# RWKV-7 mixer in a hybrid trunk: one 128x128 transpose for alpha and v, and two heads that alternate

## The chip, the cores and the metric

The kernel runs on one core of a Trainium2 chip. The metric is the device time of one execution in microseconds. Times are medians of several runs; the trace is of one profiled execution.

## The reference

One inference step of a trunk with two layers, for 1024 latent and 128 context tokens (1152 in all), model width 1024, float32. Each layer projects the normed input for four parallel groups of heads, joins their outputs in one projection, and ends with a squared-ReLU MLP. One of the groups is the RWKV-7 mixer, 4 heads of 64, run forward and backward over the tokens. Per token, with a state S (value x key) for each head, it is this scan:

```python
def step(S, inp):
    r_t, w_t, kk_t, a_t, kt_t, v_t = inp
    s_kk = jnp.einsum('bhvk,bhk->bhv', S, kk_t)
    S = (S * w_t[:, :, None, :] - s_kk[..., None] * (kk_t * a_t)[:, :, None, :]
         + v_t[..., None] * kt_t[:, :, None, :])
    return S, jnp.einsum('bhvk,bhk->bhv', S, r_t)
```

The other groups are a bidirectional SSD, neighbourhood attention and differential attention.

## The kernel before, in words

The mixer works in chunks of 64 tokens: 18 chunks, 16 latent and 2 context. Two heads share the 128 partitions (a head pair p, 64 channels each), so there are two pairs, two directions d and two layers: eight passes. `rwkv_first` builds for one pass the tiles A and B of 128 x 18 x 2 x 64 (of each chunk: in A alpha and the decayed r, in B beta and the decayed k) and the small triangular matrices Ti, which a solver on 72 partitions (lines 861 to 868, VectorE and GpSimd) inverts block by block and `rwkv_join` completes. `rwkv_second` is the pass itself. `prepare` takes a group of four chunks (the last group, of the context, has two), `scan` carries the state over them.

`prepare` runs, with PSUM tiles of one bank each from `ps3`: the transposes of v and of alpha into one bank (lines 930 and 931: v by a product with the identity into partitions 64 to 127, alpha by a transpose into partitions 0 to 63), emptied by ScalarE into R (lines 932, 933); for each head four products of B with A (line 938, the head's 64 partitions as contraction) into a bank of its own, masked by VectorE into E (line 939); the transposes of B (line 942); products of E with R (947), of R with Ti (952) and of E with R again (958), each emptied by ScalarE or VectorE. In float32 a product leaves two records, a transpose one.

`ps3` hands out tiles of a pool of two banks, and each third one from the pool `ps_e` of one bank, until that pool is given up after the first of a layer's four passes. `values` loads v of a head pair (128 x 1152) from scratch memory by SyncE's queue, once for both directions.

The program is written in an order, and a planner puts each engine's instructions in the order in which it expects them to be ready, earlier ones in the program first. So neighbourhood attention (`nat_core`, lines 1174 to 1257) and differential attention (`diff_core`, lines 1274 to 1380), which come later in the program, fill TensorE between the mixer's steps: their scores are lines 1231, 1232 and 1347, their transposes and value products lines 1129 and 1141. Each engine works through its own list in order.

Of the kernel before, what the change touches and what calls it, by code (L numbers as in the profile page):

```python
# [8 lines left out]
F32 = mybir.dt.float32  # L9
# [3 lines left out]
ALU = mybir.AluOpType  # L13
# [5 lines left out]
T = NS + NP_  # L19
# [11 lines left out]
def bcast_mid(ap, n):  # L31
    return ap.unsqueeze(1).to_broadcast([ap.shape[0], n, ap.shape[1]])
# [79 lines left out]
def ps2(env):  # L112
    return env.ps_d.tile([128, 512], F32, tag="d", name="psd")


def ps3(env):

    env.turnr += 1
    if env.ps_e is not None and env.turnr % 3 == 0:
        return env.ps_e.tile([128, 512], F32, tag="e", name="pse")  # L120
    return ps2(env)
# [567 lines left out]
def rwkv_core(env, u, a, b, st0, scr, yout, stout):  # L689

    nc, C = env.nc, env.const
    big = u.big2

    u.St = [[[[big.tile([128, 64], F32, name=f"st{q}{s}{h}{i}") for i in range(3)] for h in range(2)] for s in range(2)] for q in range(2)]
    for q in range(2):
        for s in range(2):
            for h in range(2):
                for i in range(3):
                    lo = 64 - 64 * h
                    nc.gpsimd.tensor_copy(u.St[q][s][h][i][lo:lo + 64, :], C.idst[lo:lo + 64, :])  # L700

    u.R = [big.tile([128, 4, 256], F32, name=f"R{i}") for i in range(2)]
    for r in u.R:
        nc.gpsimd.memset(r[64:128, :, 0:64], 0.0)
        nc.gpsimd.memset(r[64:128, :, 192:256], 0.0)
    u.turn = 0

    def values(p):
        u.vv = big.tile([128, T], F32, tag="vv", name="vv")
        nc.sync.dma_start(out=u.vv, in_=scr[7 + p])  # L710
        u.yf = big.tile([128, T], F32, tag="yf", name="yf", bufs=2)

    first = lambda p, d: rwkv_first(env, u, p, d, scr, ps3)
    join = lambda d, w: rwkv_join(env, u, d, w, ps3)
    second = lambda p, d, w, *between: rwkv_second(env, u, p, d, w, st0, stout, between)
    done = []
    step = lambda f: lambda: next(f)
    last = lambda f: lambda: done.append(next(f))
    values(0)
    f = first(1, 0)  # L720
    second(0, 0, a, (0, step(f)), (1, step(f)), (2, step(f)))
    join(1, b)
    next(f)
    env.ps_e = None
    g = first(1, 1)
    second(0, 1, b, (-1, last(f)), (0, step(g)), (1, step(g)), (2, step(g)))
    y0 = u.yf
    a = done.pop()
    join(0, a)
    next(g)  # L730
    b = next(g)
    values(1)
    second(1, 0, a)
    rwkv_out(env, u, 0, y0, u.pt, scr, yout)
    join(1, b)
    second(1, 1, b)
    env.wide = True
    rwkv_out(env, u, 1, u.yf, u.pt, scr, yout, psd)
# [137 lines left out]
def rwkv_join(env, u, d, work, ps):  # L876

    nc = env.nc
    Ti, dT, dTT = work[2], work[4], work[5]
    q = d * 32  # L880
    o = 32 - q
    TU = u.FT("TU", 1152)[0:64].rearrange("p (u x) -> p u x", x=32)
    nc.sync.dma_start(out=TU[q:q + 32], in_=dT[d * 36:d * 36 + 36].rearrange("u t j -> t u j"))
    for u0 in range(0, 36, 16):
        m = min(16, 36 - u0)
        um = lambda a, m=m: a.rearrange("p (u x) -> p u x", u=m)
        pp = ps(env)
        for i in range(m):
            nc.tensor.matmul(pp[o:o + 32, i * 32:i * 32 + 32], Ti[q:q + 32, u0 + i, o:o + 32], TU[q:q + 32, u0 + i], start=True, stop=True)
        nc.scalar.activation(out=TU[o:o + 32, u0:u0 + m], in_=um(pp[o:o + 32, :m * 32]), func=AF.Copy)  # L890
    for b in range(2):
        nc.sync.dma_start(out=Ti[b * 32:b * 32 + 32, :, b * 32:b * 32 + 32], in_=dTT[b * 36:b * 36 + 36].rearrange("u j t -> j u t"))
    for u0 in range(0, 36, 16):
        m = min(16, 36 - u0)
        um = lambda a, m=m: a.rearrange("p (u x) -> p u x", u=m)
        pp = ps(env)
        for i in range(m):
            nc.tensor.matmul(pp[q:q + 32, i * 32:i * 32 + 32], TU[o:o + 32, u0 + i], Ti[o:o + 32, u0 + i, o:o + 32], start=True, stop=True)
        nc.scalar.activation(out=Ti[q:q + 32, u0:u0 + m, o:o + 32], in_=um(pp[q:q + 32, :m * 32]), func=AF.Copy)


def rwkv_second(env, u, p, d, work, st0, stout, between=()):

    nc, C, big, yf = env.nc, env.const, u.big2, u.yf
    A, B, Ti, sc = work[:4]
    u.turn += 1
    St = u.St[u.turn % 2]
    for s in range(2):
# [14 lines left out]
    def prepare(gi):  # L923
        c0, m = groups[gi]
        R = u.R[gi % 2]
        E = big.tile([128, 2, 4, 192], F32, tag="E", name="E", bufs=2)
        cm = lambda a: a.rearrange("p (c x) -> p c x", c=m)
        pp = ps3(env)
        for i in range(m):
            nc.tensor.matmul(pp[64:128, i * 128:i * 128 + 128], u.vv[:, (c0 + i) * 64:(c0 + i) * 64 + 64], C.ident, start=True, stop=True)  # L930
            nc.tensor.transpose(pp[0:64, i * 128:i * 128 + 128], A[:, c0 + i, 0], C.ident)
        nc.scalar.activation(out=R[64:128, 0:m, 64:192], in_=cm(pp[64:128, :m * 128]), func=AF.Copy)
        nc.scalar.activation(out=R[0:64, 0:m].rearrange("p c (a x) -> p c a x", a=4)[:, :, 0:4:3], in_=pp[0:64, :m * 128].rearrange("p (c a x) -> p c a x", c=m, a=2), func=AF.Copy)
        for h in range(2):
            hs = slice(h * 64, h * 64 + 64)
            pp = ps3(env)
            for i in range(m):
                nc.tensor.matmul(pp[:, i * 128:i * 128 + 128], B[hs, c0 + i].rearrange("p a t -> p (a t)"), A[hs, c0 + i].rearrange("p a t -> p (a t)"), start=True, stop=True)  # L938
            nc.vector.tensor_tensor(out=E[:, h, 0:m, 0:128], in0=cm(pp[:, :m * 128]), in1=bcast_mid(C.mask[d], m), op=ALU.mult)
        pp = ps3(env)  # L940
        for i in range(m):
            nc.tensor.transpose(pp[:, i * 128:i * 128 + 128], B[:, c0 + i].rearrange("p a t -> p (a t)"), C.ident)
        nc.scalar.activation(out=E[:, :, 0:m, 128:192].rearrange("p h c x -> p c h x"), in_=pp[:, :m * 128].rearrange("p (c h x) -> p c h x", c=m, h=2), func=AF.Copy)
        pp = ps3(env)
        for i in range(m):
            for h in range(2):
                nc.tensor.matmul(pp[0:64, i * 128 + h * 64:i * 128 + h * 64 + 64], E[64:128, h, i, 0:64], R[64:128, i, 64 + h * 64:128 + h * 64], start=True, stop=True)
        nc.scalar.activation(out=R[0:64, 0:m, 64:192], in_=cm(pp[0:64, :m * 128]), func=AF.Copy)
        pp = ps3(env)
        for i in range(m):  # L950
            for h in range(2):
                nc.tensor.matmul(pp[h * 64:h * 64 + 64, i * 128:i * 128 + 128], Ti[:, h * 18 + c0 + i], R[:, i, h * 128:h * 128 + 128], start=True, stop=True)
        for h in range(2):
            nc.scalar.activation(out=R[0:64, 0:m, h * 128:h * 128 + 128], in_=cm(pp[h * 64:h * 64 + 64, :m * 128]), func=AF.Copy)
        for h in range(2):
            pp = ps3(env)
            for i in range(m):
                nc.tensor.matmul(pp[:, i * 128:i * 128 + 128], R[:, i, h * 128:h * 128 + 128], E[:, h, i, 64:192], start=True, stop=True)  # L958
            pv = cm(pp[:, :m * 128])
            z, w = slice(h * 64, h * 64 + 64), slice(64 - h * 64, 128 - h * 64)  # L960
            nc.vector.tensor_tensor(out=E[z, h, 0:m, 64:128], in0=pv[z, :, 0:64], in1=A[z, c0:c0 + m, 1], op=ALU.add)
            nc.vector.tensor_tensor(out=E[z, h, 0:m, 128:192], in0=pv[z, :, 64:128], in1=bcast_mid(C.idst[z], m), op=ALU.add)
            nc.scalar.activation(out=E[w, h, 0:m, 64:192], in_=pv[w], func=AF.Copy)
        return E
# [31 lines left out]
    def also(gi):  # L996
        for g, f in between:
            if g == gi:
                f()

    E = prepare(0)
    also(-1)
    for gi in range(5):
        nxt = prepare(gi + 1) if gi < 4 else None
        scan(gi, E)
        also(gi)
        E = nxt
# [725 lines left out]
```

## Time and profile before

| | |
|---|---|
| time, median of 3 runs | 4233.19 us (4231.91 to 4238.97) |
| time of the profiled execution | 4236.38 us |
| its span | 4234.6 us |
| TensorE busy | 4062.3 us, 96% of the span |
| VectorE busy | 2498.9 us, 59% |
| ScalarE busy | 1524.2 us, 36% |
| GpSimd busy | 1104.4 us, 26% |
| mean granted TensorE clock | 0.965 of 2.4 GHz |

A timeline row gives start, duration, engine, line, operation and tiles (written <- read) of one or several equal instructions in a row; in brackets stands the idle time of the engine before it and what ended it. PE is TensorE, DVE VectorE, ACT ScalarE, POOL GpSimd, SPq the queue of SyncE, which issues the DMAs. A product's duration includes its drain, so neighbours overlap; what it costs the engine's list is the distance from start to start.

### The profile page before, as it was taken

How to read it: one execution, taken by the hardware profiler on the slowest of the kernel's cores; microseconds unless marked ns; L12 is line 12 of the kernel's file. 1: busy time of each engine (PE TensorE's matmuls, PEld its weight loads, DVE VectorE, ACT ScalarE, POOL GpSimd, SP SyncE). 2: the span in 40 equal slices, each digit the busy share in tenths (PEclk: the TensorE clock that was granted, in tenths of full speed). 3: DMA queues.
4: the chain of work that ended last, by engine and by line, in shares of the span. 5: the costliest groups of instructions: out<-in, count | busy, mean ns of one | idle time of the engine just before them, and what ended most of it. 6: DMA issues, size and time to landing. Idle time of an engine off the chain costs nothing.

```text
span 4234.6 us, 69159 instructions
## 1 busy us (share of the span) xinstructions
PE 4062.3 (96%) x27394; PEld 3722.1 (88%) x27394; DVE 2498.9 (59%) x5734; ACT 1524.2 (36%) x2896; POOL 1104.4 (26%) x866
## 2 busy tenths in 40 slices
PE   8899889999989999999999999899999999999999
PEld 5889877777779999999998998778777999999999
DVE  4896747678675894333345756576877463333333
ACT  4333325556553212211243233355566241111111
POOL 2243340223133221111232433302322331211111
PEclk9999989989999999999999998999889999999999
DMA  6663343322221451111134333543221301111111
GB/s 196 199 199 112 121 133 76 84 64 68 54 96 54 145 169 60 40 46 40 41 110 147 119 127 95 143 97 83 41 60 46 135 26 40 43 42 40 45 41 70
DMA packets 222707, 375.74 MB, mean 89 GB/s; under 512 B 100960, under 2 KB 155760, under 8 KB 221360
## 3 DMA queue, kind: packets, MB, share of 16 engines
q1 hardware_dynamic: 222320, 371.31, 29.2%
q8 instruction: 216, 3.54, 0.4%
q14 instruction: 107, 0.88, 0.1%
q0 software_dynamic: 64, 0.02, 0.0%
HBM read 285.33 MB, written 86.42 MB: 88 GB/s over the span
## 4 chain that ended last, share of the span: by engine, by line
PE 77%; DVE 11%; DMA 5%; issue 2%; SPq 2%; ACT 2%; POOL 1%; DVEq 0%; ACTq 0%; POOLq 0%
PE psd L101 12%; PE psd L99 12%; PE psd L100 12%; PE tps L1141 5%; PE psx L101 5%; PE psx L99 5%; PE psx L100 5%; PE tps L1129 3%; PE S L1347 2%; DVE junk L162 2%; PE psd L938 1%; DVE tm L867 1%; PE psd L958 1%; PE psd L930 1%; DMA K<-scr 1%
## 5 line engine op out<-in xcount | busy, mean ns | idle before, releaser
L84 POOL TENSOR_TENSOR wl<-raw,wh 128x1024 fp32r<-128x1024 f32 (+3 forms) x200 | 474.2, 2372 | 1543.1 <-ACT wh L82 1520.5
L82 ACT ACTIVATE wh<-raw 128x1024 fp32r<-128x1024 f32 (+3 forms) x200 | 205.9, 1031 | 793.8 <-PE psd L101 672.7
L294 DVE SCALAR_TENSOR_TENSOR x<-psd,md,x 128x384 f32<-128x384 f32 (+2 forms) x442 | 212.5, 504 | 349.5 <-PE psd L101 346.0
L101 PE MATMUL psd<-fl,wh 128*128 128x384 f32 x992 | 335.2, 338 | 0.0
L99 PE MATMUL psd<-fh,wl 128*128 128x384 f32 x992 | 334.7, 337 | 0.0
L100 PE MATMUL psd<-fh,wh 128*128 128x384 f32 x992 | 334.6, 337 | 0.0
L99 PE MATMUL psd<-h2h,wl 128*128 128x384 f32 x816 | 283.5, 348 | 9.1 <-ACT st L262 6.2
L1141 PE MATMUL tps<-pT,V 128*64 128x128 f32 (+1 forms) x2144 | 287.8, 284 | 4.5 <-ACT pT L1136 3.7
L100 PE MATMUL psd<-h2h,wh 128*128 128x384 f32 x816 | 282.7, 347 | 0.0
L101 PE MATMUL psd<-h2l,wh 128*128 128x384 f32 x816 | 281.3, 346 | 0.0
L1141 PEld LDWEIGHTS tps<-pT,V 128*64 128x64 f32 (+1 forms) x2144 | 239.1, 141 | 36.2 <-issue 22.8
L379 DVE TENSOR_TENSOR fl<-s,fh 128x384 fp32r<-128x384 f32 x192 | 209.1, 1090 | 97.4 <-ACT fh L378 97.0
L1136 ACT ACTIVATE pT<-tps 128x512 f32<-128x512 f32 (+3 forms) x368 | 166.3, 475 | 173.6 <-PE tps L1129 160.6
L99 PE MATMUL psd<-h0h,wl 128*128 128x384 f32 x592 | 207.5, 350 | 0.8 <-ACT qx L1098 0.6
L377 DVE SCALAR_TENSOR_TENSOR s<-psd,r 128x384 f32<-128x384 f32 x128 | 71.2, 556 | 231.2 <-ACT r L376 230.8
L99 PE MATMUL psd<-h1h,wl 128*128 128x384 f32 x592 | 205.3, 347 | 2.4 <-ACT h1h L244 2.0
L100 PE MATMUL psd<-h0h,wh 128*128 128x384 f32 x592 | 204.9, 346 | 0.0
L100 PE MATMUL psd<-h1h,wh 128*128 128x384 f32 x592 | 204.3, 345 | 0.0
L101 PE MATMUL psd<-h0l,wh 128*128 128x384 f32 x592 | 203.8, 346 | 0.0
L101 PE MATMUL psd<-h1l,wh 128*128 128x384 f32 x592 | 202.2, 343 | 0.1
L294 DVE SCALAR_TENSOR_TENSOR x<-psx,md,x 128x384 f32<-128x384 f32 (+2 forms) x198 | 103.4, 538 | 160.6 <-PE psx L101 160.2
L1353 ACT ACTIVATE e<-e,st 128x1280 f32<-128x1280 f32 x144 | 180.5, 1253 | 47.4 <-DVE st L1352 40.6
(613 smaller groups left out, 11021.3 us busy)
## 6 DMA issues: line engine op xcount, KB each, us to landing
raw<-in_w_ff_dram SPq DMA_DIRECT2D x128, 512.0 KB
mod<-in_w_mod_dram SPq DMA_DIRECT2D x80, 512.0 KB
raw<-in_w_in_fm_dram SPq DMA_DIRECT2D x42, 512.0 KB
scr<-st SPq DMA_DIRECT2D x78, 192.0 KB
scr<-x SPq DMA_DIRECT2D x26, 576.0 KB
K<-scr SPq DMA_DIRECT2D x32, 352.0 KB
K<-scr SPq DMA_DIRECT2D x64, 176.0 KB
u<-scr SPq DMA_DIRECT2D x18, 576.0 KB
```

The lines of the kernel that those rows point to most:

```text
L82: nc.scalar.activation(out=h[:, :n], in_=raw, func=AF.Copy)
L84: nc.gpsimd.tensor_tensor(out=l[:, :n], in0=raw, in1=h[:, :n].bitcast(F32), op=ALU.subtract)
L99: nc.tensor.matmul(ps, al, bh, start=i == 0, stop=False)
L100: nc.tensor.matmul(ps, ah, bh, start=False, stop=False)
L101: nc.tensor.matmul(ps, ah, bl, start=False, stop=i == n - 1)
L162: nc.vector.scalar_tensor_tensor(out=junk, in0=w[:, i * 512:i * 512 + 512], scalar=0.5, in1=parts[c * 2 + i], op0=ALU.mult, op1=ALU.mult, ...
L294: env.nc.vector.scalar_tensor_tensor(out=x[:, kt, s0:s1], in0=ps[:, s0 - c0:s1 - c0], scalar=g[:, kt, cd:cd + 1], in1=x[:, kt, s0:s1], op0 ...
L379: nc.vector.tensor_tensor(out=fl[j][:, c0:c0 + n], in0=s, in1=fh[j][:, c0:c0 + n].bitcast(F32), op=ALU.subtract)
L1129: nc.tensor.transpose(pp[0:n, i * 128:i * 128 + 128], e[:, o:o + n], C.ident)
L1136: nc.scalar.activation(out=pT[0:g[i][1], i * 128:j * 128], in_=pp[0:g[i][1], i * 128:j * 128], func=AF.Copy)
L1141: nc.tensor.matmul(out, V[0:n, vb], parts[k // 4][0:n, k % 4 * 128:k % 4 * 128 + 128], start=k == 0, stop=k == len(kt) - 1)
L1353: nc.scalar.activation(out=e[:, :N], in_=e[:, :N], func=AF.Exp, scale=-1.0, bias=m, accum_out=st[:, 6:7] if c else s0)
```

## The change

Alpha and v of a chunk stand side by side in one tile `av` of 128 x 18 x 2 x 64. v is loaded straight into its half; alpha is copied into the other half by GpSimd at the start of each pass, from A, which keeps its own. One transpose of 128x128 a chunk takes the place of the product and the transpose. The products of the two heads are issued in turn, chunk by chunk, into two banks that are taken together, and the two masks follow.

```diff
     def values(p):
-        u.vv = big.tile([128, T], F32, tag="vv", name="vv")
-        nc.sync.dma_start(out=u.vv, in_=scr[7 + p])
+        u.av = big.tile([128, 18, 2, 64], F32, tag="av", name="av")
+        nc.sync.dma_start(out=u.av[:, :, 1], in_=scr[7 + p].rearrange("p (c t) -> p c t", t=64))
...
     A, B, Ti, sc = work[:4]
+    av = u.av
+    nc.gpsimd.tensor_copy(av[:, :, 0], A[:, :, 0])
...
         for i in range(m):
-            nc.tensor.matmul(pp[64:128, i * 128:i * 128 + 128], u.vv[:, (c0 + i) * 64:(c0 + i) * 64 + 64], C.ident, start=True, stop=True)
-            nc.tensor.transpose(pp[0:64, i * 128:i * 128 + 128], A[:, c0 + i, 0], C.ident)
+            nc.tensor.transpose(pp[:, i * 128:i * 128 + 128], av[:, c0 + i].rearrange("p a t -> p (a t)"), C.ident)
...
+        pair = [ps3(env), ps3(env)]
+        for i in range(m):
+            for h in range(2):
+                hs = slice(h * 64, h * 64 + 64)
+                nc.tensor.matmul(pair[h][:, i * 128:i * 128 + 128], B[hs, c0 + i].rearrange("p a t -> p (a t)"), A[hs, c0 + i].rearrange("p a t -> p (a t)"), start=True, stop=True)
         for h in range(2):
-            hs = slice(h * 64, h * 64 + 64)
-            pp = ps3(env)
-            for i in range(m):
-                nc.tensor.matmul(pp[:, i * 128:i * 128 + 128], B[hs, c0 + i].rearrange("p a t -> p (a t)"), A[hs, c0 + i].rearrange("p a t -> p (a t)"), start=True, stop=True)
-            nc.vector.tensor_tensor(out=E[:, h, 0:m, 0:128], in0=cm(pp[:, :m * 128]), in1=bcast_mid(C.mask[d], m), op=ALU.mult)
+            nc.vector.tensor_tensor(out=E[:, h, 0:m, 0:128], in0=cm(pair[h][:, :m * 128]), in1=bcast_mid(C.mask[d], m), op=ALU.mult)
```

## Rows read from the trace of the kernel before

**Rows 1.** Both stretches: length; PE, PEld, DVE, ACT, POOL busy; clock; DMA share, GB/s

```profile
628.00:1250.00 622.00, 580.49 (x5001) 463.61 (x4999) 449.21 (x1168) 353.43 (x698) 140.14 (x151) 0.94 0.29 72
2694.00:3310.00 616.00, 579.58 (x5008) 464.06 (x5007) 453.46 (x1165) 353.83 (x696) 150.95 (x164) 0.93 0.32 79
```

**Rows 2.** The chain that ended last, shares by line, 628 to 1250 us

```profile
by line: PE tps L1141 16.9%; PE tps L1129 7.8%; PE S L1347 5.3%; PE psd L938 5.0%; issue 4.0%; PE psd L958 3.9%; PE psd L930 3.1%; DMA K<-scr 3.0%; PE psd L947 2.5%; PE S L1231 2.3%; PE psx L979 2.3%; PE psd L931 2.0%; PE S L1232 1.8%; PE p
```

**Rows 3.** TensorE's timeline in a group of layer 1's last pass

```profile
3211.09 0.43 PE L930 MATMUL psd<-pack,vv 128*64 128x128 f32 x2
...
3211.68 0.43 PE L930 MATMUL psd<-pack,vv 128*64 128x128 f32 x2
...
3212.86 1.16 PE L938 MATMUL psd<-A,B 64*128 64x128 f32 x8
3213.95 0.66 PE L1129 MATMUL tps<-pack,e 128*128 128x128 f32 x4
...
3215.34 1.16 PE L938 MATMUL psd<-A,B 64*128 64x128 f32 x8
3216.42 0.66 PE L942 MATMUL psd<-pack,B 128*128 128x128 f32 x4
3216.84 0.48 PE L1347 MATMUL S<-K,Q 128*128 128x512 f32 x1
```

**Rows 4.** TensorE's timeline, a group of two chunks with both heads together

```profile
2811.87 0.37 PE L938 MATMUL psd<-A,B 64*128 64x128 f32 x1
2811.89 0.37 PE L938 MATMUL pse<-A,B 64*128 64x128 f32 x1
...
2812.53 0.39 PE L1231 MATMUL S<-K,Q 128*128 128x256 f32 x1
```

**Rows 5.** TensorE's timeline, a group whose heads stand one behind the other

```profile
688.40 0.82 PE L938 MATMUL pse<-A,B 64*128 64x128 f32 x5
...
690.04 0.33 PE L942 MATMUL psd<-pack,B 128*128 128x128 f32 x1
```

**Rows 6.** ScalarE's timeline, the second eviction of the transposes of rows 3

```profile
3213.57 0.59 ACT L933 ACTIVATE R<-psd 64x512 f32<-64x512 f32 x1
```

**Rows 7.** Timeline at the start of layer 1's stretch: GpSimd, and the first transposes

```profile
2697.14 2.41 POOL L852 TENSOR_TENSOR A<-r,W 128x1152 f32<-128x1152 f32 x1
...
2699.61 8.28 POOL L700 COPY st<-pack 64x64 f32<-64x64 f32 x24
...
2708.70 0.31 POOL L705 MEMSET R<- 64x256 f32 x1
...
2710.22 0.69 PE L930 MATMUL pse<-pack,vv 128*64 128x128 f32 x2
...
2714.85 0.66 POOL L1211 COPY BI<-BT 128x576 f32<-128x576 f32 x1 [5.85 <-DMA BT<-scr]
```

**Rows 8.** Line 930 alone between passes: length, PE busy (records), clock, DMA

```profile
739.00:762.00 23.00, 0.00 (x0) 0.93 0.77 197
...
869.00:904.00 35.00, 0.00 (x0) 0.76 0.50 138
```

**Rows 9.** SyncE's timeline: issues of v's load and of a load in 256-byte runs

```profile
2697.92 0.57 SPq L710 DMA_DIRECT2D vv<-scr  x1
...
2700.78 0.60 SPq L1202 DMA_DIRECT2D V<-scr  x1
```

**Rows 10.** Longest pieces of layer 1's chain: start, us, what

```profile
2697.92 5.99 DMA vv<-scr
2703.93 10.78 DMA BT<-scr
```

**Rows 11.** Stretches of 40 us, columns as in rows 1

```profile
880.00:920.00 40.00, 33.11 (x343) 26.46 (x339) 28.42 (x86) 16.31 (x29) 6.35 (x6) 0.71 0.36 83
...
3160.00:3200.00 40.00, 40.00 (x362) 32.76 (x361) 31.76 (x82) 26.89 (x47) 7.15 (x6) 1.00 0.05 11
3200.00:3240.00 40.00, 36.72 (x336) 30.83 (x334) 25.72 (x69) 26.11 (x52) 5.78 (x4) 1.00 0.39 96
```

## Prediction

> **What bounds the kernel now.** The change touches two stretches, one in each layer, in which the RWKV mixer runs beside neighbourhood and differential attention: from its first transposed chunk to the last value products, 628 to 1250 us and 2694 to 3310 us. I read the busy time of each engine there first [rows 1]: TensorE is busy for 580.49 of 622 us and 579.58 of 616 us, so it stands idle for 41.5 and 36.4 us, 78 of 1238 us (6%). VectorE follows with 449 and 453 us. The reader is to see that no other engine comes near TensorE. Second, the chain of work that ended last [rows 2]: in layer 0's stretch it runs over TensorE's lines, attention's L1141 and L1129 first, with L938 at 5.0%, L930 at 3.1% and L931 at 2.0%. So these products of the mixer are not hidden work: they stand in one queue with attention's products. Third, the order of TensorE's instructions in time, because busy time counts the drain of each product beside the start of the next: what one costs the queue is the distance from its start to the next start [rows 3].
>
> **Part one: one transpose for two.** Now each chunk takes a product of v with the identity (two records) and a transpose of alpha; they repeat every 0.59 us (3211.09 to 3211.68; three such periods and a little reach to 3212.86) [rows 3]. There are 18 chunks, 4 passes (two head pairs, two directions) and 2 layers: 144 chunks, 144 x 0.59 = 85 us. After it a chunk is one 128x128 transpose against the identity. The same form stands at L942: four take 0.42 us from the first start to the next line's start (3216.42 to 3216.84), 0.105 us each [rows 3]. A group pays something for changing from one kind of product to another; I take 0.14 us a chunk, 20 us. Saved: 65 us of TensorE's queue. At the lower clock both grow alike, so that is no smaller there. The eviction by ScalarE stays: two instructions with the same shapes.
>
> **Part two: the heads alternate.** One head's four products (K 64, so half of the array's rows; two records each) hold the queue for 1.09 us (3212.86 to 3213.95), and the other head's for 1.08 (3215.34 to 3216.42) [rows 3]. Where both heads' products were ready together, they ran side by side already: in one group of two chunks the records start in pairs, 2811.87 and 2811.89, and both heads are through by 2812.53, 0.66 us with the change of kind at either end [rows 4]. Where one head's block stands right before the other's, they overlap in part: sixteen records in 1.64 us, 688.40 to 690.04 [rows 5]. So if the alternation reaches the engine, a group of four saves about 1.09 us and one of two about 0.44: 32 x 1.09 + 8 x 0.44 = 38 us, less some 4 us that such groups have now, 34. If it doesn't, 0. What decides is the second PSUM bank: the pair now wants two at once, and for most of the stretch (after ps_e is given up) the pool has two, of which the transposes just before hold one until ScalarE has emptied it, to 3213.57 + 0.59 = 3214.16, while the first head started at 3212.86 [rows 3, 6]. An order made by readiness would then run head 0's four products first. I take half, 17 us, and keep 0 and 34 for the range. VectorE's two masks come after both heads instead of one after each; the first waits longer by one head's products at most, and the second follows it as now.
>
> **Part three: the copy.** GpSimd gets one copy of 128 x 1152 a pass, 8 in all. No row has one of that size: the 128x576 copy took 0.66 us, a 128x1152 product of two tensors 2.41 us [rows 7], so it lies between 1.3 (twice the first) and 2.4; I take 1.6, nearer to the copy, because it also has one input. GpSimd has room, 140 of 622 us busy [rows 1]. What counts is when it ends. It overwrites half of a tile with one buffer, so it waits for the transposes of the pass before; behind it in GpSimd's queue stand the solver's products and attention's scalings. Between the last transposes of a pass and the first of the next lie 23 us in one place and 35 us in another without any [rows 8], so the copy has time, unless it stands behind a GpSimd instruction that itself waits. Only at the start of a layer's stretch is there no room: GpSimd makes 24 small copies from 2699.61 on and ends its memsets at 2708.70 + 0.31, and the first transposes come at 2710.22 [rows 7]. A copy of 1.3 to 2.4 us ends between 2710.3 and 2711.4, 0.1 to 1.2 us late.
>
> **Part four: the load of v.** It is the same 576 KB by one instruction on SP, but in runs of 256 bytes instead of whole rows. Another load in runs of 256 bytes (L1202) issues in 0.60 us against 0.57, so what is queued behind it, the state z and attention's Q and K, moves by next to nothing [rows 9]. Its landing is not shown. v's load took 5.99 us on the chain; the load of BT, 224 KB in runs of 256 bytes, 10.78 us, queued behind others [rows 10]. Between no change and 576/224 x 10.78 = 27.7 us, thus 0 to 22 us more, twice (the second pair's load starts some 35 us before its use [rows 8]). As v landed at 2703.9 and was used at 2710.22 [rows 7, 10], the first 6 us of that are covered. I take 1.5 us a layer for copy and load together, 3 us in all; the upper end is 2 x 16 = 32. The Trainium skill ("DMA: Bandwidth & Descriptors", the table at its head) says that transfers under 512 bytes fall below line rate, which speaks against this load. By it the upper end would be the likelier one, and the time 29 us later than by the value that I take; no row here times such a load alone.
>
> **The sum.** TensorE's queue gets 65 + 17 = 82 us shorter. The stretch gives back less, since in 6% of it something else ends last and the softmax chain of VectorE and ScalarE does not shrink; I take four fifths, 66 us (bounds: all, and half). Less 3: 63. The profiled execution took 4236.4 us (its span 4234.6), 3.2 above the median of the three runs. 4236.4 - 63 = 4173, and against the median 4170 us.
>
> **The rivals.** *All of it comes back* (chance 0.15): the mixer's own chain gets shorter by the same products, and attention fills every gap; with the pairs kept, 65 + 34 = 99 us, 4134. For it: the chain runs over TensorE [rows 2]. Against it: the idle time that is there now.
> *The pairs don't alternate and half is lost* (0.12): the second head waits for its bank, so the change does only half of what it says, and with TensorE freed the softmax chain, VectorE at 449 us [rows 1], ends last more often: 65 / 2 - 3 = 30 us, 4203.
> *The start of each layer's stretch eats it* (0.06): the load of 256-byte runs lands late by its upper bound, 32 us, on top of a halved gain of 32: 4233, no change.
> *The clock* (0.07, slower). The granted clock was 0.94 and 0.93 in the two stretches [rows 1]: mostly 2.4 GHz, at times 1.2. It fell where TensorE was idle, 0.71 with 33.11 of 40 us busy, and stayed at 1.00 where it was busy throughout [rows 11]. The change takes products away and leaves transposes, and leaves TensorE idle more often. Each 0.01 of mean clock costs 12 us over 1238 us, so from a fall of 0.05, to 0.885, the 63 us are gone; at 0.85 it would be 105 - 63 = 42 us slower, 4275. The stretch keeps hundreds of us of attention's products, so I hold it for unlikely. The Trainium skill ("TensorE: Matmul & The Clock Gate", Part 4) says that transposes don't count as busy time for the clock; by that rule this case would be likelier. The trace doesn't bear that out so far: the stretch with the transposes of [rows 3] stands at 1.00 with 36.72 of 40 us busy [rows 11], though none is of transposes alone.
>
> **How the numbers follow.** The forecast, 4170, has 0.60 with its own range of 4150 to 4192; the rivals 0.15, 0.12, 0.06 and 0.07. Eight in ten lie from 4130 to 4212: the best case and the halved one are in, no change and the clock are out. A measurement of this kernel can tell about 0.2%, 8.5 us, from no change. Faster: forecast, best case, halved case, 0.87; within 0.2%: 0.06; slower: 0.07.
>
> **What would show it.** The period of 0.59 us is gone, and groups of four 128x128 transposes stand in its place in 0.4 to 0.6 us. Both heads' records start in pairs, sixteen in about 1.1 us; if eight of one head stand before eight of the other, part two is worth nothing. TensorE's busy time in the two stretches falls by some 80 us and its idle time rises by less than 20. The first transposes of a layer come at most 2 us later in the stretch. I am wrong if the stretches keep their length while TensorE's idle time grows by what its work lost, or if the granted clock falls under 0.9.

## The result, and the profile after

The changed kernel takes 4427.77 us (median of 4 runs, 4420.3 to 4430.64), the kernel before 4232.55 us beside it (4 runs): 195 us or 4.6% slower, ratio 1.0457 with a 95% interval of 1.0444 to 1.047. The profiled execution of after has a span of 4425.2 us at a mean granted clock of 0.935. The forecast was 4170 us, with a range of 4130 to 4212 and a chance of 0.07 for slower.

The loss lies in the two stretches of the prediction and nowhere else. ScalarE's splits of the projection weights (line 82) follow in the same order in both kernels: the 45th of them starts at 1414.1 us before and at 1511.8 after (+97.7), the 105th, still ahead of layer 1's stretch, at 2201.6 and 2299.4 (+97.8), the 161st, behind it, at 3674.6 and 3865.2 (+190.6), the 201st at 4180.2 and 4370.8 (+190.6). Each layer loses about 95 us.

The busy times of the engines from the first score product of neighbourhood attention to the last one of differential attention (columns as in [rows 1]). Before:

```profile
633.00:1221.00 588.00, 552.54 (x4813) 440.20 (x4812) 426.63 (x1124) 337.14 (x670) 124.54 (x124) 0.94 0.27 64
2707.00:3304.00 597.00, 567.76 (x4870) 453.40 (x4870) 440.52 (x1140) 350.91 (x688) 136.45 (x140) 0.93 0.30 73
```

After:

```profile
630.00:1388.00 758.00, 655.33 (x5132) 546.43 (x5133) 461.02 (x1176) 357.03 (x698) 149.31 (x144) 0.86 0.26 67
2812.00:3551.00 739.00, 652.19 (x5119) 542.57 (x5119) 460.76 (x1174) 357.00 (x697) 156.25 (x144) 0.87 0.27 69
```

Against [rows 1] no engine took over: VectorE, ScalarE and GpSimd have about the work that they had. TensorE stands idle for 103 and 87 us, 35 and 29 before, and its clock is 0.86 and 0.87 instead of 0.94 and 0.93. Nothing is the bound any more; something waits. The windows of after hold more than those of before: the projection that joins the groups now starts beside attention, and its products with the tile `mh` are busy in them for 75.82 and 77.17 us, before for 0 and 9.83. So the stretches grow by 170 and 142 us while a layer loses about 95. What waits is seen in the score products of differential attention alone (before L1347, after L1351), layer 0, the columns being PE busy (records), PEld busy (records), clock, DMA share and GB/s. Before:

```profile
880.00:1080.00 200.00, 41.66 (x109) 19.86 (x109) 0.89 0.26 60
1080.00:1400.00 320.00, 29.18 (x91) 14.97 (x91) 0.99 0.21 68
```

After:

```profile
880.00:1080.00 200.00, 0.00 (x0) 0.00 (x0) 0.67 0.10 28
1080.00:1400.00 320.00, 68.04 (x197) 34.94 (x197) 0.92 0.27 74
```

Before, differential attention runs beside the mixer's second head pair. After, it does not begin until the mixer is through, and in the 200 us in between the clock is 0.67. The mixer itself is faster: its last scan product starts at 1059 us instead of 1187. But the mixer's last two passes (891 to 1059) and attention (1089 to 1388) now stand one behind the other, 168 + 299 us, where both together took 339 (882 to 1221). After, the change from the mixer to attention on SyncE's queue, and then on TensorE:

```profile
1075.99 4.18 SPq L771 DMA_DIRECT2D scr<-yf  x3
1080.35 0.33 SPq L1273 DMA_DIRECT2D Q<-scr  x1
1080.73 0.42 SPq L1274 DMA_DIRECT2D K<-scr  x1
```

```profile
862.28 0.82 PE L1351 MATMUL S<-K,Q 128*128 128x512 f32 x3
...
1088.71 1.41 PE L1351 MATMUL S<-K,Q 128*128 128x512 f32 x3 [11.27 <-DMA K<-scr]
```

Three products of the first half of a head were made at 862; the load of Q for its second half (each head of differential attention has two) is issued right behind the mixer's last stores, 218 us later. The chain of what ended last reaches back over only 18% of the span of after, so [rows 2] has no counterpart.

What the load waits for is seen in neither trace but in where the planner placed the buffers. The mixer's tiles grow upward from one side of a partition's memory, attention's downward from the other:

```
bytes of a partition              before             after
E, second buffer                  150176 to 156320   154784 to 160928
fin (final state)                 156320 to 156576   160928 to 161184
gst (norm of the mixer's output)  156576 to 156792   161184 to 161400
Q of attention's second half      159264 to 163872   159264 to 163872
```

`av` is 9216 bytes a partition where `vv` was 4608. Before, 2472 bytes were free between gst and Q; after, gst, fin and part of E lie in Q's place, by 2136 bytes. So Q's load must wait for the last use of E, fin and gst, which is the end of the mixer, and in SyncE's list it stands behind the mixer's stores.

The steps of the prediction themselves, in after. TensorE in a group of the last pass [rows 3]:

```profile
3217.73 0.66 PE L933 MATMUL psd<-pack,av 128*128 128x128 f32 x4 [0.25 <-ACT E L967]
3218.64 1.16 PE L941 MATMUL psd<-A,B 64*128 64x128 f32 x8 [0.26 <-ACT E L967]
...
3220.11 1.16 PE L941 MATMUL psd<-A,B 64*128 64x128 f32 x8
3221.19 0.66 PE L946 MATMUL psd<-pack,B 128*128 128x128 f32 x4
```

and in the group that [rows 5] showed:

```profile
687.41 1.16 PE L941 MATMUL pse<-A,B 64*128 64x128 f32 x8
688.50 0.43 PE L1145 MATMUL tps<-pT,V 128*64 128x128 f32 x2
688.86 1.16 PE L941 MATMUL psd<-A,B 64*128 64x128 f32 x8
```

Four transposes stand in place of twelve records. The heads do not alternate: eight records of one and then eight of the other, with other work between. Of the 576 records of this line in the trace, 18 start within 25 ns of the one before (24 before the change). GpSimd and SyncE at the start of a layer's stretch [rows 7, 9], with SyncE's two rows of before in a fence of their own:

```profile
2811.28 1.14 POOL L908 COPY av<-A 128x1152 f32<-128x1152 f32 x1
```

```profile
618.26 0.59 SPq L711 DMA_DIRECT2D av<-scr  x1
618.90 3.81 SPq L915 DMA_DIRECT2D z<-in_st_rwkv_dram  x1
622.76 0.45 SPq L1202 DMA_DIRECT2D Q<-scr  x1
```

```profile
620.15 0.58 SPq L710 DMA_DIRECT2D vv<-scr  x1
620.77 0.43 SPq L912 DMA_DIRECT2D z<-in_st_rwkv_dram  x1
```

The copy took 1.14 us. The load of v issues in 0.59 us, but the small load behind it in the queue took 3.81 us to issue where it took 0.43. The trace of before has the like behind attention's load of V, also in runs of 256 bytes, in the row that follows the second one of [rows 9]:

```profile
2701.42 1.64 SPq L1203 DMA_DIRECT2D V<-in_nat_cv_dram  x1
```

Where another load stood between the two, the same line took 0.57 us (2710.52).

### The profile page after: what moved, and what is told of

Read it like the earlier page. It is cut to its first block, busy times and chain, and to the rows that moved or that the text cites. A ratio compares the mean times of both kernels' runs of the same rounds, so it can differ in the third digit from the quotient of the medians.

```text
span 4425.2 us, 68721 instructions
## 1 busy us (share of the span) xinstructions
PE 4100.1 (93%) x27106; PEld 3770.9 (85%) x27106; DVE 2510.5 (57%) x5734; ACT 1521.0 (34%) x2896; POOL 1109.3 (25%) x874
## 5 line engine op out<-in xcount | busy, mean ns | idle before, releaser
L84 POOL TENSOR_TENSOR wl<-raw,wh 128x1024 fp32r<-128x1024 f32 (+2 forms) x200 | 477.4, 2387 | 1571.1 <-ACT wh L82 1546.1
L82 ACT ACTIVATE wh<-raw 128x1024 fp32r<-128x1024 f32 (+2 forms) x200 | 206.1, 1030 | 712.7 <-PE psd L101 620.8
L1133 PE MATMUL tps<-pack,e 128*128 128x128 f32 (+1 forms) x1072 | 181.2, 293 | 11.9 <-ACT pT L1140 4.1
```

Source lines behind the costliest of these rows:

```text
L82: nc.scalar.activation(out=h[:, :n], in_=raw, func=AF.Copy)
L84: nc.gpsimd.tensor_tensor(out=l[:, :n], in0=raw, in1=h[:, :n].bitcast(F32), op=ALU.subtract)
L1133: nc.tensor.transpose(pp[0:n, i * 128:i * 128 + 128], e[:, o:o + n], C.ident)
```

## The experiments

The theory: the time is lost to the 2136 bytes. Rival A: the new products, their order or the clock cost it. Rival B: the copy and the load cost it at the start of a stretch. Each ratio is to runs of the kernel before on the same chip beside it, with its 95% interval.

**The memory alone.** Three kernels are the kernel before with a longer buffer for v, of which only the old part is used:

```diff
-        u.vv = big.tile([128, T], F32, tag="vv", name="vv")
+        u.vv = big.tile([128, T + 1152], F32, tag="vv", name="vv")[:, 0:T]
```

with 1152, 576 and 640 columns more (4608, 2304 and 2560 bytes).

> The kernel before, with 4608 more bytes per partition in the buffer of v and nothing else; the added columns are never used. Memory theory (the larger buffer makes the mixer's pool reach into the place where differential attention's Q of its second head is loaded, by 2136 bytes per partition, so this load and the attention behind it wait for the mixer's last pass): about 4420 us, and TensorE's products of differential attention begin after the mixer's last pass, near 1090 us, instead of near 880. Rival A (the transposes, the order of the heads or the lower clock cost the time): 4233, unchanged. Rival B (the copy on GpSimd and the load of v in short runs at the start of each layer's stretch cost it): 4233, unchanged.

(What it calls the Q of the second head is the Q of the second half of a head.)

Measured: 4464.73 us, ratio 1.0561 [1.0535, 1.0587].

> The kernel before, with 2304 more bytes per partition in the buffer of v: the mixer's pool then ends 168 bytes short of differential attention's Q. Memory theory: 4233, unchanged, as nothing overlaps. If any growth of the pool costs time by itself (another way for buffers to be shared): between 4233 and 4420. Rivals A and B: 4233.

Measured: 4230.24 us, ratio 1.0001 [0.9986, 1.0016].

> The kernel before, with 2560 more bytes per partition in the buffer of v: the pool ends 88 bytes behind the beginning of differential attention's Q, so only the last small tile of the mixer (gst, used when the mixer's output is normalised) shares bytes with it. Memory theory: as late as with 4608 bytes or a little later, as the last user of gst stands at the very end of the mixer, 4420. Rivals A and B: 4233.

Measured: 4460.49 us, ratio 1.0553 [1.0529, 1.0577]. Attention's score products in the same two windows, first with 4608 bytes, then with 2560, then with 2304:

```profile
880.00:1080.00 200.00, 0.82 (x3) 0.49 (x3) 0.77 0.12 35
1080.00:1400.00 320.00, 67.62 (x197) 35.30 (x197) 0.91 0.27 75
```

```profile
880.00:1080.00 200.00, 0.82 (x3) 0.49 (x3) 0.76 0.11 32
1080.00:1400.00 320.00, 68.18 (x197) 35.69 (x197) 0.91 0.27 75
```

```profile
880.00:1080.00 200.00, 40.38 (x112) 19.40 (x112) 0.91 0.26 63
1080.00:1400.00 320.00, 29.04 (x89) 14.91 (x89) 0.98 0.21 68
```

With 2304 bytes more the pool ends 168 bytes short of Q, and the time does not move. With 256 bytes above that, gst, a tile of 216 bytes, shares 88 bytes with Q, and 5.5% are lost, as much as with all 4608 bytes. The loss is a step and not a slope. No product, copy or load of the change is in these kernels, so A and B cannot explain it. Where the buffer lies matters as little: with 2304 and with 2560 bytes more all that follows `vv` in the pool has moved, and only the second loses time. That these two cost 236 and 231 us and the change 195 fits a change that saves something and pays for the overlap.

**The change with room.** In `after_st1` the recurrence has one set of state tiles instead of two, which two passes in a row share:

```diff
-    u.St = [[[[big.tile([128, 64], F32, name=f"st{q}{s}{h}{i}") for i in range(3)] for h in range(2)] for s in range(2)] for q in range(2)]
+    u.St = [[[[big.tile([128, 64], F32, name=f"st{q}{s}{h}{i}") for i in range(3)] for h in range(2)] for s in range(2)] for q in range(1)]
...
-    St = u.St[u.turn % 2]
+    St = u.St[0]
```

> The changed kernel with one set of the recurrence's state tiles instead of two, which takes 3072 bytes per partition out of the mixer's pool: it then ends 936 bytes short of differential attention's Q. All the rest of the change stays. Memory theory: attention runs beside the mixer again, and what the transposes save shows: 4233 less 65 x 0.8 and 3 more for the copy and the load, about 4185, from 4165 to 4200 (a little later if the single set makes a pass wait for the one before). Rivals A and B: 4428, as late as the changed kernel.

Measured: 4185.22 us, ratio 0.9904 [0.9878, 0.993]. Attention runs beside the mixer again:

```profile
880.00:1080.00 200.00, 41.16 (x112) 20.43 (x112) 0.86 0.20 49
1080.00:1400.00 320.00, 27.56 (x82) 13.45 (x82) 0.99 0.25 80
```

So 3072 bytes turn a loss of 195 us into a gain of about 41 (0.96%). The control is the kernel before with the same one set:

> The kernel before with one set of the recurrence's state tiles, nothing else (control for after_st1, whose 4185 us then stand against this kernel). GpSimd then makes 12 small copies at the start of each layer's stretch instead of 24, 5.75 us less, and a pass may have to wait for the states of the pass before. If all of after_st1's gain of 44 us is the transposes': 4229, unchanged. If the shorter start is part of it: up to 2 x 5.75 = 11 us faster, 4218. If the single set holds passes up: slower than 4233, and the transposes are worth more than 44 us.

Measured: 4248.37 us, ratio 1.0039 [1.0021, 1.0057]. The smaller set costs this kernel time (about 16 us by the ratio), so the change is worth more than it shows against the kernel before: 0.9904 / 1.0039 = 0.9866, 57 us.

**Its parts.** `tr_st1` has the transposes, the copy and the load, and the heads one behind the other as before. `pairf_st1` is `after_st1` with each product of the pair put behind the one before it by an explicit order, so that the heads must alternate:

```diff
+        prev = None
         for i in range(m):
-            for h in range(2):
+            for h in (1, 0):
                 hs = slice(h * 64, h * 64 + 64)
-                nc.tensor.matmul(pair[h][:, i * 128:i * 128 + 128], B[hs, c0 + i].rearrange("p a t -> p (a t)"), A[hs, c0 + i].rearrange("p a t -> p (a t)"), start=True, stop=True)
+                with ExitStack() as behind:
+                    if prev is not None:
+                        behind.enter_context(env.tc.issue_after(prev))
+                    prev = nc.tensor.matmul(pair[h][:, i * 128:i * 128 + 128], B[hs, c0 + i].rearrange("p a t -> p (a t)"), A[hs, c0 + i].rearrange("p a t -> p (a t)"), start=True, stop=True).ins
```

> The changed kernel's transposes, copy and load with the heads one after the other as before, and one set of state tiles. Against after_st1 it shows what the alternation of the heads is worth as it stands. Theory (the second bank of PSUM comes free too late, both heads' products still stand in blocks of eight records, so the alternation is worth nothing): 4185 us within 8. Rival (it is worth the 17 us that I took, part of the products being side by side): 4202.

Measured: 4186.95 us, ratio 0.9881 [0.9865, 0.9897].

> after_st1 with the alternation made sure: each of the heads' products is put behind the one before it in TensorE's order, so that records of both heads start in pairs. If side by side they take half the time, as one group of the kernel before did (16 records in 0.66 us with the change of kind at both ends, against 1.09 + 1.08 us for 32), TensorE's queue gets 34 us shorter and the time falls by half to four fifths of that: 4158 to 4168. Rival (the group now waits for two free banks at once, and what the products gain is lost in that wait): 4185, or a little slower, up to 4200.

(The group of the kernel before has 8 records in 0.66 us, and the other two blocks have 16 together; the proportion stands.)

Measured: 4183.39 us, ratio 0.9877 [0.986, 0.9893]. A group in `tr_st1`, and one in `pairf_st1`:

```profile
658.10 0.60 PE L933 MATMUL pse<-pack,av 128*128 128x128 f32 x4
658.63 0.54 PE L1144 MATMUL tps<-pT,V 128*64 128x128 f32 x3
```

```profile
690.86 0.58 PE L945 MATMUL psd<-A,B 64*128 64x128 f32 x1
690.86 0.58 PE L945 MATMUL pse<-A,B 64*128 64x128 f32 x1
691.23 0.42 PE L945 MATMUL psd<-A,B 64*128 64x128 f32 x1
691.24 0.42 PE L945 MATMUL pse<-A,B 64*128 64x128 f32 x1
```

All of the gain comes with the transposes, the copy and the load, which `tr_st1` has. As written the alternation gains nothing (0.9904 with it, 0.9881 without, with intervals that overlap). Forced, the records start in pairs, and the line holds TensorE's queue for 61 us where it held it for 85 in `tr_st1` (all 576 records of the trace, from start to next start, idle time left out); the time does not follow. What comes in its place is waiting. The two stretches of `tr_st1`, then of `pairf_st1`:

```profile
634.00:1214.00 580.00, 546.32 (x4762) 449.36 (x4762) 440.25 (x1142) 350.11 (x691) 141.51 (x134) 0.92 0.30 74
2679.00:3242.00 563.00, 523.78 (x4673) 429.40 (x4673) 430.62 (x1133) 341.77 (x681) 128.18 (x132) 0.93 0.30 72
```

```profile
635.00:1206.00 571.00, 527.99 (x4740) 434.62 (x4741) 436.66 (x1141) 350.70 (x690) 142.97 (x134) 0.92 0.31 75
2679.00:3252.00 573.00, 529.39 (x4726) 432.57 (x4727) 437.27 (x1140) 349.17 (x690) 144.16 (x135) 0.92 0.31 76
```

TensorE's idle time is 73 us in the first and 87 in the second; both are 1143 to 1144 us long.

**The load of v.** Its landing could hold up the first transposes of a layer. In `after` and `after_st1` these come 8 to 14 us behind the first score product of neighbourhood attention, before 4 us ahead of it in one layer and 3 us behind in the other. `ldsplit_st1` is `after_st1` with two loads, the first of four chunks:

```diff
-        nc.sync.dma_start(out=u.av[:, :, 1], in_=scr[7 + p].rearrange("p (c t) -> p c t", t=64))
+        v = scr[7 + p].rearrange("p (c t) -> p c t", t=64)
+        nc.sync.dma_start(out=u.av[:, 0:4, 1], in_=v[:, 0:4])
+        nc.sync.dma_start(out=u.av[:, 4:18, 1], in_=v[:, 4:18])
```

> after_st1 with the load of v split in two, the first four chunks in a load of their own. In after_st1 the copy on GpSimd ends 10 us ahead of the first transposes of each layer (629.5 against 638.5, 2679.2 against 2689.4). If the landing of the long load of 256-byte runs is what they wait for, they come some 5 to 8 us earlier in a layer and the time falls by up to 2 x 6 = 12 us, to 4173 to 4180. If something else holds them (the order of TensorE's queue, loads of attention), unchanged, 4185.

Measured: 4194.87 us, ratio 0.99 [0.9885, 0.9915]; the first transposes come at 642 us, no earlier (638 in `after_st1`). The landing is not what they wait for, and the trace of after tells when it was: the last of the load's 2304 packets of 256 bytes ends at 624.9 us at the latest, 6.6 us after the issue, and in layer 1 at 2806.8, 7.0 us after it (5.99 before [rows 10]). The first transposes start at 644.4 and 2825.2. `tr_actq` is `tr_st1` with v's loads issued by ScalarE:

```diff
-        nc.sync.dma_start(out=u.av[:, :, 1], in_=scr[7 + p].rearrange("p (c t) -> p c t", t=64))
+        nc.scalar.dma_start(out=u.av[:, :, 1], in_=scr[7 + p].rearrange("p (c t) -> p c t", t=64))
```

> tr_st1 with the loads of v issued by ScalarE instead of SyncE. If the stall belongs to the queue in which the 256-byte runs stand: the load of the initial state issues in 0.4 us again, attention's first K lands some 3.5 us earlier in each layer, and the time falls from 4187 by up to 2 x 3.5 = 7 us, 4180. Rival (the stall moves to ScalarE, or the transfers hold each other up wherever they are issued): 4187 or some us more.

Measured: 4189.09 us, ratio 0.9888 [0.9868, 0.9907]. SyncE and then TensorE in `tr_actq`, and TensorE in `tr_st1`:

```profile
623.10 0.58 SPq L915 DMA_DIRECT2D z<-in_st_rwkv_dram  x1
```

```profile
640.35 0.80 PE L1234 MATMUL S<-K,Q 128*128 128x512 f32 x1 [3.88 <-DVE st L1241]
...
641.95 1.06 PE L933 MATMUL psd<-pack,av 128*128 128x128 f32 x4
```

```profile
640.80 0.80 PE L1234 MATMUL S<-K,Q 128*128 128x512 f32 x1 [2.32 <-DVE st L1241]
...
642.39 1.06 PE L933 MATMUL psd<-pack,av 128*128 128x128 f32 x4
```

With the load on the other queue the stall behind it is gone from SyncE's, and no gain is seen (the two ratios could tell one of about 10 us): the transposes stand in TensorE's list behind attention's score products, and these wait for VectorE's softmax, 1.56 us longer now.

**Room made in other ways.** One set of states costs something of its own, so the room was made twice more, with both sets of the long recurrence kept. In both, the short recurrence (two chunks) has its zero state written once and one tile for the other state. In `fit` the initial state is loaded in place besides; in `fit2` gst shares fin's buffer instead. The core of `fit2`:

```diff
+    one = [[st(f"one{i}", 1, h) for i in range(2)] for h in range(2)]
+    u.St = [[[[st(f"st{q}{i}", 0, h) for i in range(3)] for h in range(2)], one] for q in range(2)]
...
-    st = u.big2.tile([128, 3, 18], F32, tag="gst", name="gst")
+    st = u.big2.tile([128, 64], F32, tag="fin", name="fin")[:, 0:54].rearrange("p (a b) -> p a b", a=3)
```

and of `fit`:

```diff
-            z0 = big.tile([128, 64], F32, tag="z0", name="z0")
-            nc.sync.dma_start(out=z0, in_=st0[d, p])
...
+                nc.sync.dma_start(out=St[s][h][0][z, :], in_=st0[d, p][z])
```

> The kernel before with 2304 bytes per partition less in the mixer's pool and both sets of the long recurrence's state kept: the short recurrence's zero state is written once, its other state has one tile, and the initial state is loaded in place. Control for the next three. The single set of before_st1 cost 11.6 us, by waiting theory because the next pass's writes to it stood on VectorE behind the pass before; here no pass waits, and GpSimd makes 16 small copies instead of 24 at a layer's start: 4237 or up to 8 us faster. Rival (less memory in this pool costs time by itself): 4248, as before_st1.

> The changed kernel whole (transposes, copy, load, order of the heads), with the same 2304 bytes taken out of the mixer's pool, which then ends 168 bytes short of differential attention's Q. If the transposes are worth what tr_st1 against before_st1 says (4187 - 4248 = -61 us): 4233 less 61, 4172. Rival (they are worth the 44 to 50 us by which after_st1 and tr_st1 beat the kernel before, and the single set's cost belongs to before_st1 alone): 4185.

> As fit, but with the heads one behind the other as in the kernel before. If their order as written in the change is worth nothing, as tr_st1 against after_st1 said: within 8 us of fit, 4172. If it is worth the 17 us of my sum: 4189.

> As fit, with the records of the two heads put in turns by force. In pairf_st1 TensorE spent 24 us less on these products and the time moved by 4 us at most. If the gain is eaten by waits for two free banks: 4172, as fit. If it was only hidden by the single set of states: 4172 less half of 24, 4160.

> The kernel before, with 2264 bytes less in the mixer's pool: the short recurrence's zero state is written once and its other state has one tile, and the small tile of the output's normalisation shares the buffer of the final state. The initial state is loaded as in the kernel before. Control. If the loads in place cost before_fit its 6 us: 4233 or some us faster (16 small copies on GpSimd instead of 24 at the start of a layer's stretch). If the shared short state costs them: 4239.

> The whole change with this room. If the delayed start cost fit its gain: 4233 less 44 to 61, so 4172 to 4189. If the transposes with two sets of long states are worth no more than in fit: 4210 to 4216.

> As fit2 with the heads one behind the other. Within 9 us of fit2 if the order as written is worth nothing (tr_fit was 9 us faster than fit, tr_st1 within 4 us of after_st1 by the ratios); 17 us slower than fit2 if it is worth what my sum took.

> As fit2 with the records of the heads in turns by force. If the alternation, once it is on the engine, is worth what pairf_fit showed against fit: 30 us less than fit2, 4145 to 4160. If it was worth that only because fit's clock and start were bad: as fit2.

Measured, each as a ratio to the kernel before with its interval:

| room made by | kernel before | whole change | heads one behind the other | heads in turns by force |
|---|---|---|---|---|
| one set of states (st1) | 1.0039 [1.0021, 1.0057] | 0.9904 [0.9878, 0.993] | 0.9881 [0.9865, 0.9897] | 0.9877 [0.986, 0.9893] |
| states loaded in place (fit) | 1.0017 [1.0008, 1.0026] | 0.9961 [0.9948, 0.9974] | 0.9938 [0.9925, 0.9951] | 0.9886 [0.9872, 0.9901] |
| shared small tiles (fit2) | 1.0034 [1.0024, 1.0045] | 0.9896 [0.9879, 0.9913] | 0.9897 [0.9881, 0.9914] | 0.9902 [0.9883, 0.992] |

In all nine kernels of the table that have the transposes and room for them, the time is below the kernel before. With room by st1 and by fit2 the results agree: the whole change 0.9866 and 0.9862 of its control (57 and 58 us), the heads' order worth nothing, forced or not, as far as the intervals can tell. With `fit` the gain is only 24 us (0.9944 of its control), and the forced alternation is worth 22 to 32 there. I had put `fit`'s shortfall down to its four loads of states, which hold SyncE for 5.87 us ahead of attention's first Q and K. `fit2` against `fit` speaks for that, but the controls speak against it: `before_fit`, with the same loads, is no slower than `before_fit2`. Why `fit` gains less, and why the kernel before loses 0.2 to 0.4% when its pool gets smaller, is left open; the order of TensorE's list differs in all of them, and what each difference is worth was not measured.

The best of these beat both kernels: with the transposes and one set of states 4183 to 4187 us, 1.0 to 1.2% below the kernel before.

## Why the prediction was wrong

**The step that failed is the overlap, which the prediction took as given.** Its first paragraph finds the mixer running "beside neighbourhood and differential attention", and its sum has no term for what could end that. The change's list was costed as instructions: two products out, a transpose in, a copy, a load. That `av` is twice as large as `vv` stands in the diff, and the prediction put it at nothing without a reason. It costs 231 to 236 us by the pads, more than three times the 63 us that it forecast for all the edits. What it would have taken stands in the kernel's description: attention fills TensorE between the mixer's steps, which it can only do while its buffers don't lie where the mixer's are. The question to ask is which bytes that takes, and how many are free beside them: 2472, against 4608 asked for.

**Part one, the transposes, was right in kind and in size.** A chunk's records held the queue for 0.59 us by [rows 3], and over all 144 chunks (the records of the two lines, from start to next start, idle time left out) for 88 us: the 85 of the sum. After, a group of four takes 0.53 us (658.10 to 658.63 above), 0.13 a chunk, and all 144 take 21.3 in `tr_st1` where I had taken 20. Part of the gain goes again elsewhere: the heads' products behind them hold the queue for 85.1 us in `tr_st1` and 78.0 in `before_st1`. The queue gets 65 - 7 = 58 us shorter by these lines, and the time of `tr_st1` against its control falls by 0.9881 / 1.0039 = 0.9843, 66 us (some 10 either way). I had let four fifths of the queue's gain through; with this room all of it comes through, as far as the interval tells, and with `fit`'s only 33 us do (0.9938 / 1.0017).

**Part two's 17 us are 0.** The lower bound held: the trace shows one head's products run ahead of the other's, as an order made by readiness would put them; that the second bank is what comes late was argued and not measured. But a shorter queue was no shorter time either. With the order forced in `pairf_st1` the queue gets 24 us shorter and the time stays: 14 us come back as idle time of TensorE, and the stretches keep their length. Only with `fit`'s room does the forced order gain, 22 to 32 us, and why there is open.

**Parts three and four were right in sum and wrong in mechanism.** The copy took 1.14 us, less than my lowest, 1.3, and ends ahead of the first transposes. Yet these come 11 and 18 us later in the stretches of `after`, and not at most 2: in TensorE's list they now stand behind attention's score products. The load of v I costed by its own issue, 0.60 against 0.57 us, and concluded that what is queued behind it moves by next to nothing. At the start of a layer the issue right behind it takes 3.6 to 4.5 us (`after`, `after_st1`, `tr_st1`, `pairf_st1`) where it took 0.43; the row behind L1202, with its 1.64 us, was a sign of that in the trace of before, and I did not read it. No cost in time is seen: `tr_actq`, without the stall, is no faster. The page "DMA: Bandwidth & Descriptors" of the Trainium skill (its table at the head) has transfers under 512 bytes below line rate. By it the upper end of the load's cost would have been the likelier one. That end did not come: the load landed 6.6 and 7.0 us after its issue, against 5.99 before, and the trace has the cost in the queue instead.

**The rivals.** The one on the slower side was the clock: it fell, to 0.86 and 0.87, below the 0.9 that I had named. But it fell with attention gone from TensorE, 0.67 in the 200 us in which the mixer ran alone, and in the pads as well (0.77, 0.76), which have no transpose more than before. With the transposes and room it is 0.92 and 0.93 (`tr_st1`). So it is a part of the price of the overlap and not its cause. The page "TensorE: Matmul & The Clock Gate" of the Trainium skill (Part 4) says that transposes don't count as busy time in the way of products. What the runs have on it is the 0.92 and 0.93 with the larger transposes against 0.94 and 0.93 before, and the 0.67 against 0.77 in the pad of 4608, where TensorE was busy for 160.65 and 170.81 of the 200 us; what part of these differences the transposes have is not shown. Of the two signs that I had named, the clock under 0.9 came. The other came by half: TensorE's idle time grew from 65 us to 190 in the two stretches, but these grew as well, by 170 and 142 us, for a reason that was not on the list.

**The forecast, were there room,** was 63 us. Against their controls the kernels with room show 57 and 58, in `fit` 24; against the kernel before as it stands, 41 to 44, and 17 in `fit`. So in two of the three ways to make room it was the right size for the part that it looked at, and that in part by luck: 49 us from the transposes that were 58 to 66 there, and 14 from the alternation that were 0.

## What to carry to other kernels

A diff that makes a buffer larger has a price that no row of the trace of before shows: look at where the buffer ends and what begins there, and ask which later stage runs early only because its buffers are free. The price is a step: 168 bytes of room cost nothing, 88 bytes of overlap 5.5%. A long idle time of an engine with all others as busy as before, and a load issued right behind another stage's last store, is how it looks in a profile; and two padded buffers in the old kernel, one that just overlaps and one that just does not, tell it apart from everything else.

## What the hardware showed

A load of 576 KB in 2304 runs of 256 bytes issued in 0.59 us, as fast as one in 128 rows of 4608 bytes (0.58), but the next load on the same queue needed 3.81 us to issue instead of 0.43; with the large load on ScalarE's queue it was 0.58. The short runs did not make the load late: it had landed 6.6 us after its issue, against 5.99 on the chain of before. Two products of 64 rows each, one in either half of the array, start within 10 ns of each other when both heads' records are put in turns, as in the pairs from 690.86 us on. That this frees 24 us of TensorE's queue and nothing of the time (`pairf_st1` against `tr_st1`) was not expected.
